# Layer 0's first shift and scale by TensorE in four column tiles instead of VectorE

## The chip, the cores and the metric

One core of a Trainium2 chip runs the whole program. The metric is the device time of one execution in microseconds (us); lower is better. Engines are called as the profile calls them: PE (TensorE) with its weight loads PEld, DVE (VectorE), ACT (ScalarE), POOL (GpSimd) and SP (SyncE, which here only issues transfers). Each engine runs its own instructions in its own order and waits on semaphores for the others. Transfers are issued by SP, ACT and POOL; each of the three has its own queue on the same 16 DMA engines (q1 for SP, q10 for ACT, q0 for POOL).

## What is computed

A two-layer encoder over 256 tokens of width 1024, conditioned on a vector `c`. Only the start matters here:

```python
mod = jnp.einsum('bd,lde->lbe', jax.nn.silu(c), w_ada) + b_ada[:, None, :]
for layer in range(DEPTH):
    shift1, scale1, gate1, shift2, scale2, gate2 = jnp.split(mod[layer][:, None, :], 6, axis=-1)
    h = x * (1.0 + scale1) + shift1
    y = hybrid_mixer(h, positions, w_in[layer], w_out[layer], ...)
    x = layer_norm(DEEPNORM_ALPHA * x + (1.0 + gate1) * y, ln_w[layer, 0], ln_b[layer, 0])
    h = x * (1.0 + scale2) + shift2
    f = swiglu(...) if layer % 2 == 0 else moe_swiglu(...)
    x = layer_norm(DEEPNORM_ALPHA * x + (1.0 + gate2) * f, ln_w[layer, 1], ln_b[layer, 1])
```

For each layer six vectors of 1024 (shift, scale and gate, twice) are products of `silu(c)` with a 1024 x 6144 matrix. Layer 0 cannot begin its first projection before its first shift and scale (pieces 0 and 1) are there, and they take 8 MB of weights.

## The kernel before

**Tiles and names.** 128 partitions hold 128 tokens or 128 of the 1024 features. `x` holds both token blocks b = 0, 1. The features are taken in two halves q = 0, 1 of four blocks of 128 each. All large weights come through four buffers of 1 MB (`raw`, tag "raw", `RAW = 4`), in the order in which SP issues them; a load waits until the buffer's last reader is done.

**The vectors.** `ada_steps` makes shifts and scales on DVE. `sc` is `c` broadcast to all partitions and put through Silu by ACT. One step loads 1 MB of transposed weights (two blocks of 128 outputs) and DVE multiplies each block by `sc` and sums along the row: one 128x1024 instruction per block of 128 outputs (L324) and one small instruction that adds the bias (L325). `feed(n)` runs n steps. For layer 0 the main loop calls `feed(4)` ahead of each half q, which makes scale and shift of that half: four loads and eight of the long DVE instructions.

**The first half-projection.** For each q: `transposed` turns `x` into features by PE (eight transposes L300 per q), `affine` applies scale and shift from PSUM (DVE and ACT in turn, L293 and L291), and `split` makes a high and a low part of the result (ACT copies the high part, L254; DVE subtracts to get the low part, L255). The weights of the projection go through the same `split`. `channels(0)` then multiplies: per half q 48 products of 128x256 (L476 to L478), three for each of four feature blocks and four output blocks. The high part alone is enough for the first product; the low part is needed from the second on. The second half q = 1 accumulates onto the first.

**Next on the path.** While the products run, DVE makes two blocks of another vector, splits weights and prepares constants; ACT then runs a chain of small activations with table loads (constants, rotary tables, the gates from the first projection) and then casts the weights of the next projection (ORDER "05...": chunk 5 follows chunk 0).

**The order.** A scheduler places the instructions of each engine in a fixed order at build time; on the chip each engine keeps that order. Within an engine, what stands behind a waiting instruction waits too.

**The routing's constants.** `moe` copies eight columns of `small` to `of` (L952), about 600 us into the program; the scheduler had moved the copy to the front of DVE's order.

Of the kernel before, what the change touches and what calls it, by code (L numbers as in the profile page):

```python
# [8 lines left out]
F32 = mybir.dt.float32  # L9
# [4 lines left out]
AF = mybir.ActivationFunctionType  # L14
# [3 lines left out]
P = 128  # L18
S = 256
NB = S // P  # L20
# [37 lines left out]
PLACES = PACKED + 2 * P  # L58
SMALL = PLACES + 3 * NE
LEVELS = (1, 2, 4, 8, 16, 32)  # L60
# [11 lines left out]
def shape_constants():  # L72
# [24 lines left out]
    small[:, PLACES + NE:PLACES + 2 * NE] = [NE * S * 2] + [-e for e in range(1, NE)]  # L97
    small[:, PLACES + 2 * NE:] = ROWS
    return {
# [7 lines left out]
def lay_out(i):  # L107
# [4 lines left out]
    o["pos"] = n["positions"].reshape(NB, P).T  # L112
    o["w_ada"] = n["w_ada"].reshape(DEPTH, D, 6, KD, P).transpose(0, 2, 3, 4, 1).reshape(DEPTH, 6, KD // 2, 2, P, D).transpose(0, 1, 2, 4, 3, 5)
    o["b_ada_c"] = n["b_ada"].reshape(DEPTH, 6, KD, P).transpose(3, 0, 1, 2)
    cols = np.arange(3072)
# [37 lines left out]
def trunk(tc, a, dbg=None):  # L153
# [37 lines left out]
    sc = work.tile([P, D], F32, name="sc")  # L191
    nc.scalar.dma_start(sc, a["c"].to_broadcast([P, D]))
    small = const.tile([P, SMALL], F32, name="small")
# [7 lines left out]
    x = const.tile([P, NB, D], F32, name="x")  # L201
    nc.scalar.dma_start(x, a["x"].rearrange("(b p) d -> p b d", p=P))
    lnc = const.tile([P, DEPTH, 2, 2, KD], F32, name="lnc")
    lbr = work.tile([P, DEPTH, NH], F32, name="lbr")
# [103 lines left out]


    A.activation(sc, sc, AF.Silu)  # L310

    mods = {}

    def ada_steps(todo):

        for l, piece, k in todo:
# [5 lines left out]
            for i in range(2):  # L322
# [4 lines left out]

    ada = ada_steps([(0, p, k) for k in range(0, KD, 2) for p in (1, 0)]
                    + [(*lp, k) for lp in ((0, 2), (0, 4), (0, 3), (0, 5), (1, 1), (1, 0), (1, 2), (1, 4), (1, 3), (1, 5))
                       for k in range(0, KD, 2)])  # L330

    def feed(n):
        for _ in range(n):
            next(ada, None)
# [611 lines left out]
    def moe(xn, cw, cb, g2):  # L946
# [4 lines left out]
        ind, gate, rank = [of[:, NB * j:NB * j + NB] for j in range(3)]  # L951
        V.tensor_copy(of[:, 4 * NB - 1], slots[:, 0:NE])  # L952
        tops = []
# [410 lines left out]
    for l in range(DEPTH):  # L1364
        hT = halves_T(f"hT{l}")
        last = {}
        for q in range(2):
            if l == 0:
                feed(4)
                cw, cb = mods[0, 1], mods[0, 0]  # L1370
            for b in range(NB):
                last[q, b] = to_T(src[b], b, q, hT, cw, cb, act=l > 0)
            if l == q == 0:
                early = load_w(a["w_in"][0, 0, 0], "win")
# [61 lines left out]
```

## Time and profile before

| | us |
|---|---|
| three runs | 1504.81, 1507.10, 1508.26 (median 1507.1) |
| the profiled execution, its own time | 1508.05 |
| its span, first to last instruction | 1505.9 |
| PE, DVE, ACT, POOL busy | 1308.8, 931.9, 646.9, 50.6 |

The profiled execution is 0.95 us above the median of the three runs, and its own time is 2.15 us longer than its span. The profile gives for each engine when an instruction began and how long it ran, and for an idle time what released the engine. PEclk is the clock that was granted to PE as a share of full speed: 1.00 is the level of 2.4 GHz and 0.50 that of 1.2 GHz. The first such record in this trace is at 33.4 us; before it the level is read from the spacing of equal products.

### The profile page before, as it was taken

Reading aid. Unit: us, or ns where it says so; the run is one execution under the profiler, and the core shown is the slowest. Engines: PE = TensorE matmul, PEld = TensorE weight load, DVE = VectorE, ACT = ScalarE, POOL = GpSimd, SP = SyncE. Lnnn points to the kernel's source line nnn. Section 1 sums busy time; section 2 is a strip of 40 time slices with the busy share of each in tenths; the row PEclk is TensorE's granted clock in tenths of the full one; section 3 lists DMA queues with packets and bytes.
Section 4 is the critical chain, followed back from the end, with each engine's and each line's share of the span. In section 5 each row is a group of like instructions: output and inputs, shape, how many; then the busy total and the mean of one; then the engine's idle time right before and its main releaser. Section 6 shows DMA issues by size and latency. Waiting matters only on the chain. (4 is left out here: it accounts for less than half of the span.)

```text
span 1505.9 us, 26044 instructions
## 1 busy us (share of the span) xinstructions
PE 1308.8 (87%) x10378; PEld 976.1 (65%) x10378; DVE 931.9 (62%) x1756; ACT 646.9 (43%) x1144; POOL 50.6 (3%) x44
## 2 busy tenths in 40 slices
PE   3699879999979999899999899989888898888884
PEld 2688757877768887676566567656666565655551
DVE  6799888888887987774343555443443555343424
ACT  2647744444445684564333334442444244333310
POOL 0000021000050000200000000000000000000000
PEclk9799989999979999799999999989999999888886
DMA  9773247899935403689999999999899999999994
GB/s 353 285 278 113 96 157 264 322 343 351 339 113 180 155 29 105 266 292 356 417 419 420 418 418 390 418 418 378 352 418 417 419 396 418 418 420 418 418 419 170
DMA packets 68753, 481.05 MB, mean 319 GB/s; under 512 B 8720, under 2 KB 8848, under 8 KB 11152
## 3 DMA queue, kind: packets, MB, share of 16 engines
q1 hardware_dynamic: 66672, 473.61, 79.6%
q0 software_dynamic: 960, 3.15, 0.7%
q10 hardware_dynamic: 992, 2.56, 0.4%
q8 instruction: 83, 1.36, 0.4%
q14 instruction: 46, 0.38, 0.1%
HBM read 478.23 MB, written 1.05 MB: 318 GB/s over the span
## 5 line engine op out<-in xcount | busy, mean ns | idle before, releaser
L255 DVE TENSOR_TENSOR pair<-rawb,pair 128x1024 fp32r<-128x1024 f32 x150 | 177.1, 1221 | 94.3 <-ACT pair L254 93.3
L254 ACT CAST pair<-rawb 128x1024 fp32r<-128x1024 f32 x150 | 149.9, 1048 | 36.2 <-DMA rawb<-m_up 20.4
L250 PE MATMUL pa<-pair,xe 128*128 128x512 f32 x336 | 139.4, 415 | 11.2 <-DVE pair L255 11.2
L249 PE MATMUL pa<-pair,xe 128*128 128x512 f32 x336 | 140.2, 417 | 9.7 <-ACT pair L254 9.2
L255 DVE TENSOR_TENSOR pair<-ring,pair 128x1024 fp32r<-128x1024 f32 x102 | 120.2, 1225 | 34.4 <-ACT pair L254 33.7
L251 PE MATMUL pa<-pair,xe 128*128 128x512 f32 x336 | 136.9, 407 | 0.0
L324 DVE CUSTOM_DVE_ANT_0 wada<-wada,sc 128x1024 f32<-128x1024 f32 x96 | 114.9, 1218 | 2.3 <-DMA wada<-w_ada 2.3
L808 ACT ACTIVATE g_act<-pa 128x256 f32<-128x256 f32 x64 | 24.6, 385 | 201.2 <-PE pa L251 201.2
L1132 PE MATMUL pa<-rawb,xl 128*32 128x128 f32 (+1 forms) x2320 | 103.7, 306 | 8.0 <-DMA rawb<-m_up 8.0
L254 ACT CAST pair<-ring 128x1024 fp32r<-128x1024 f32 x102 | 100.8, 1046 | 17.6 <-DVE rs_y L270 11.8
L1132 PEld LDWEIGHTS pa<-rawb,xl 128*32 128x32 f32 (+1 forms) x2320 | 79.4, 121 | 26.6 <-DMA rawb<-m_up 10.4
L1137 ACT COPY pk<-pa 128x128 f32<-128x128 f32 (+1 forms) x84 | 23.8, 283 | 154.3 <-PE pa L1132 154.3
L249 PEld LDWEIGHTS pa<-pair,xe 128*128 128x128 f32 x336 | 67.7, 201 | 32.1 <-ACT pair L254 13.6
L250 PEld LDWEIGHTS pa<-pair,xe 128*128 128x128 f32 x336 | 67.9, 202 | 31.3 <-DVE pair L255 17.6
L809 DVE TENSOR_TENSOR g_act<-g_act,pa 128x256 f32<-128x256 f32 x64 | 26.7, 417 | 97.6 <-ACT g_act L808 97.4
L255 DVE TENSOR_TENSOR g_l<-pb,g_h 128x256 fp32r<-128x256 f32 x64 | 27.0, 422 | 96.3 <-ACT g_h L254 96.1
L1132 PE MATMUL pa<-ring,xl 128*32 128x128 f32 (+1 forms) x1712 | 74.2, 301 | 11.1 <-DMA ring<-m_up 11.1
L251 PEld LDWEIGHTS pa<-pair,xe 128*128 128x128 f32 x336 | 67.9, 202 | 13.7
L254 ACT CAST win<-win 128x1024 fp32r<-128x1024 f32 x48 | 49.9, 1055 | 56.9 <-PE acc L251 24.0
L250 PE MATMUL pa<-wup,hTf 128*128 128x512 f32 x176 | 70.1, 398 | 2.4 <-DVE wup L255 2.4
L1132 PEld LDWEIGHTS pa<-ring,xl 128*32 128x32 f32 (+1 forms) x1712 | 56.5, 119 | 23.5 <-DMA ring<-m_up 13.9
L249 PE MATMUL acc<-pair,g_h 128*128 128x512 f32 x168 | 71.1, 423 | 0.0
(325 smaller groups left out, 2777.1 us busy)
## 6 DMA issues: line engine op xcount, KB each, us to landing
rawb<-m_up SPq DMA_DIRECT2D x129, 1024.0 KB, 13.0
ring<-m_up SPq DMA_DIRECT2D x95, 1024.0 KB, 13.1
rawb<-m_dn SPq DMA_DIRECT2D x71, 1024.0 KB, 14.4
wada<-w_ada SPq DMA_DIRECT2D x48, 1024.0 KB, 6.7
ring<-m_dn SPq DMA_DIRECT2D x41, 1024.0 KB, 14.7
win<-w_in SPq DMA_DIRECT2D x24, 1024.0 KB, 5.5
wup<-f_up SPq DMA_DIRECT2D x22, 1024.0 KB, 5.6
fdn<-f_dn SPq DMA_DIRECT2D x11, 1024.0 KB, 6.6
```

The source lines that it names most:

```text
L249: T.matmul(ps, xh, wh, start=first, stop=False)
L250: T.matmul(ps, xh, wl, start=False, stop=False)
L251: T.matmul(ps, xl, wh, start=False, stop=last)
L254: A.copy(h, src)
L255: return V.tensor_sub(lo, src, h.bitcast(F32))
L324: V.tensor_tensor_reduce(wi, wi, sc, 1.0, 0.0, ALU.mult, ALU.add, c[:, i:i + 1])
L808: A.activation(g, p[:, 0:FB], AF.Silu)
L809: V.tensor_mul(g, g, p[:, FB:2 * FB])
L1132: T.matmul(ps[n * i:n * i + n, 0:w], xr[:, k], ws[k // 4][:, c:c + w], start=k == 0, stop=k == KD - 1)
L1137: A.copy(s, ps)
```

## The change

Pieces 0 and 1 of layer 0 are no longer made by `ada_steps`. A second copy of their weights lies untransposed in `w_ada0`: one tile of 128x2048 (1 MB) holds four blocks of 128 inputs by 512 outputs. `c` comes a second time as `cc`, one column per block of 128 inputs (128x8), goes through Silu, and is repeated 32 times per block into `ccs`. `first_mods(q)` makes for piece 1, then 0: two tiles, each with four f32 products that go to four column tiles of PE, 32 output partitions each (L332); ACT copies the 128x512 sum from PSUM to `mod_s` (L334); four products with `pick`, whose column is 1 in every 32nd partition, add the four column tiles and turn the row into columns (L337, here called picks); DVE adds the bias (L338). The load of `sc`, which later vectors still need, goes behind `x` in ACT's queue; `cc` takes its place at the head. `of`'s copy is kept in program order.

```diff
@@ trunk: loads
-    nc.scalar.dma_start(sc, a["c"].to_broadcast([P, D]))
+    cc = const.tile([P, KD], F32, name="cc")
+    nc.scalar.dma_start(cc, a["c_c"])
...
     nc.scalar.dma_start(x, a["x"].rearrange("(b p) d -> p b d", p=P))
+    nc.scalar.dma_start(sc, a["c"].to_broadcast([P, D]))
+    pick = small[:, PICK:PICK + NE]
@@ vectors
+    A.activation(cc, cc, AF.Silu)
+    ccs = s1("ccs").rearrange("p (k j) -> p k j", k=KD)
+    V.tensor_copy(ccs, cc[:, :, None].to_broadcast([P, KD, QD]))
     A.activation(sc, sc, AF.Silu)
 
-    mods = {}
+    mods = {(0, p): const.tile([P, KD], F32, name=f"mod0{p}") for p in range(2)}
+
+    def first_mods(q):
+
+        for piece in (1, 0):
+            ps = bank("pa")
+            for h in range(2):
+                w = raw("wada")
+                nc.sync.dma_start(w, a["w_ada0"][q, piece, h].rearrange("p k n -> p (k n)"))
+                for i in range(4):
+                    T.matmul(ps[QD * i:QD * i + QD], ccs[:, 4 * h + i], w[:, 512 * i:512 * i + 512], start=h == 0, stop=h == 1)
+            s = s2("mod_s", "aff")
+            A.copy(s, ps)
+            pm = bank("pc")[:, 0:4 * NE].rearrange("p (j e) -> p j e", e=NE)
+            for j in range(4):
+                T.matmul(pm[:, j], s[:, j * P:(j + 1) * P], pick, start=True, stop=True)
+            V.scalar_tensor_tensor(mods[0, piece][:, 4 * q:4 * q + 4], pm[:, :, 0], float(piece), bac[:, 0, piece, 4 * q:4 * q + 4],
+                                   op0=ALU.add, op1=ALU.add)
@@
-    ada = ada_steps([(0, p, k) for k in range(0, KD, 2) for p in (1, 0)]
-                    + [(*lp, k) for lp in ((0, 2), (0, 4), (0, 3), (0, 5), (1, 1), (1, 0), (1, 2), (1, 4), (1, 3), (1, 5))
+    ada = ada_steps([(*lp, k) for lp in ((0, 2), (0, 4), (0, 3), (0, 5), (1, 1), (1, 0), (1, 2), (1, 4), (1, 3), (1, 5))
                        for k in range(0, KD, 2)])
@@ moe
-        V.tensor_copy(of[:, 4 * NB - 1], slots[:, 0:NE])
+        tc.keep_in_program_order(V.tensor_copy(of[:, 4 * NB - 1], slots[:, 0:NE]))
@@ main loop
             if l == 0:
-                feed(4)
+                first_mods(q)
                 cw, cb = mods[0, 1], mods[0, 0]
```

The order of instructions changes on PE, DVE and ACT up to the end of the first projection; behind it the only difference is `of`'s copy. SP issues the same loads in the same sequence: four weight tiles for q = 0 (called w1 to w4 below), the first projection tile, four for q = 1 (w5 to w8), the second projection tile.

ACT's instructions from the first one, before (`small` is a tile of constants, `bac` the biases, `cup` a tile that gets zeros, `win` weights of the projection, `hTf` the output of `affine`):

```order
L192 DMA sc<-c 128x1024
L194 DMA small<-k_small 128x800
L200 DMA bac<-b_ada_c 128x96
L202 DMA x<-x 128x2x1024
L310 ACT_TABLE_LOAD
L310 ACTIVATE sc<-sc 128x1024
L445 ACTIVATE cup<-small 128x15 x4
L254 CAST win_213<-win 128x1024
L254 CAST win_216<-win 128x1024
L291 ACTIVATE hTf<-pa,mod_119,mod_113 128x128 x4
```

and with the change:

```order
L197 DMA cc<-c_c 128x8
L199 DMA small<-k_small 128x808
L205 DMA bac<-b_ada_c 128x96
L207 DMA x<-x 128x2x1024
L208 DMA sc<-c 128x1024
L317 ACT_TABLE_LOAD
L317 ACTIVATE cc<-cc 128x8
L471 ACTIVATE cup<-small 128x15 x3
L320 ACTIVATE sc<-sc 128x1024
L471 ACTIVATE cup<-small 128x15
L334 COPY mod_s<-pa 128x512 x2
L298 ACTIVATE hTf<-pa,mod_96,mod_97 128x128 x2
```

The load of `sc` has moved from the first to the fifth place, and its activation now stands ahead of the two copies of `mod_s`; the casts of `win` have moved behind them.

PE's instructions from the first one, with the change (before, this place holds the 16 transposes of `x` and then the products L476 to L478 without a break; those products are L502 to L504 now):

```order
L332 MATMUL pa<-wada,ccs 32x512 x9
L337 MATMUL pc<-small,mod_s 128x8 x4
L332 MATMUL pa<-wada,ccs 32x512 x3
L307 MATMUL pa<-small,x 128x128 x2
L332 MATMUL pa<-wada,ccs 32x512 x4
L307 MATMUL pa<-small,x 128x128 x2
L337 MATMUL pc<-small,mod_s 128x8 x4
L307 MATMUL pa<-small,x 128x128 x4
L502 MATMUL acc_258<-hT_116,win_262 128x256
L332 MATMUL pa<-wada,ccs 32x512 x4
L503 MATMUL acc_258<-hT_117,win_262 128x256
L504 MATMUL acc_258<-hT_116,win_262 128x256
```

The first picks stand ahead of three products of w3, of all of w4's and of the transposes, and the products of w5 already stand between the first and the second product of the projection.

PE at the end of the projection's first half, with the change (before, nothing but the products L476 to L478 stands here):

```order
L332 MATMUL pa<-wada,ccs 32x512 x4
L504 MATMUL acc_259<-hT_116,win_265 128x256
L502 MATMUL acc_260<-hT_116,win_265 128x256
L503 MATMUL acc_260<-hT_117,win_265 128x256
L504 MATMUL acc_260<-hT_116,win_265 128x256
L502 MATMUL acc_261<-hT_116,win_265 128x256
L503 MATMUL acc_261<-hT_117,win_265 128x256
L337 MATMUL pc<-small,mod_s 128x8 x4
L307 MATMUL pa<-small,x 128x128 x4
L504 MATMUL acc_261<-hT_116,win_265 128x256
L502 MATMUL acc_258<-hT_118,win_318 128x256
L502 MATMUL acc_259<-hT_118,win_318 128x256
```

The products of w8, the last weight tile, and the last four picks stand behind all but a handful of the 48 products of the first half.

## Rows read from the trace of the kernel before

**Rows 1.** Busy time by stretch: PE, PEld, DVE, ACT, POOL, PEclk, DMA share, GB/s.

```profile
15.00:20.00 5.00, 0.00 (x0) 0.00 (x0) 5.00 (x11) 0.00 (x0) 0.00 (x0) 1.00 1.01 418
...
640.00:900.00 260.00, 243.71 (x1749) 165.86 (x1748) 131.29 (x185) 109.30 (x176) 0.00 (x0) 1.00 0.97 391
```

**Rows 2.** Timeline of the start: start us, duration us, engine, line, [idle before, releaser].

```profile
0.73 0.41 ACTq L192 DMA_DIRECT2D sc<-c  x1
...
8.09 1.06 ACT L310 ACTIVATE sc<-sc 128x1024 f32<-128x1024 f32 x1 [3.82 <-DMA sc<-c]
13.09 0.53 ACT L445 ACTIVATE cup<-small 128x15 fp32r<-128x15 f32 x4 [3.94 <-DMA small<-k_small]
13.09 0.17 DVE L952 COPY of<-small 128x8 f32<-128x8 f32 x1 [11.95 <-DMA small<-k_small]
```

**Rows 3.** Timeline from the first half's vectors to its first product.

```profile
23.36 1.94 PE L300 MATMUL pa<-small,x 128*128 128x128 f32 x8 [23.36 <-DMA x<-x]
...
24.82 0.15 DVE L325 SCALAR_TENSOR_TENSOR mod<-mod,bac 128x2 f32<-128x2 f32 x1
...
28.59 1.29 DVE L255 TENSOR_TENSOR hT<-hTf,hT 128x512 fp32r<-128x512 f32 x2
...
29.38 0.78 PE L476 MATMUL acc<-hT,win 128*128 128x256 f32 x2
```

**Rows 4.** Timeline from the second half's last vector instruction to the next projection.

```profile
39.82 0.15 DVE L325 SCALAR_TENSOR_TENSOR mod<-mod,bac 128x2 f32<-128x2 f32 x1
...
42.63 1.29 DVE L255 TENSOR_TENSOR hT<-hTf,hT 128x512 fp32r<-128x512 f32 x2
...
43.17 1.01 PE L476 MATMUL acc<-hT,win 128*128 128x256 f32 x3 [5.97 <-ACT hT L254]
...
48.24 0.40 ACT L684 ACTIVATE dg<-small,conv_w 128x128 fp32r<-128x128 f32 x1 [2.93 <-DVE conv_w L255]
...
58.18 3.92 ACT L254 CAST win<-win 128x1024 fp32r<-128x1024 f32 x4
```

**Rows 5.** DMA of the first 24 us: total; SP's queue; issues (KB each, us to landing).

```profile
DMA packets 1745, 8.73 MB, mean 364 GB/s; under 512 B 320, under 2 KB 320, under 8 KB 1024
...
q1 hardware_dynamic: 801, 5.91, 62.7%
...
x<-x ACTq DMA_DIRECT2D x1, 1024.0 KB, 21.1
...
sc<-c ACTq DMA_DIRECT2D x1, 512.0 KB, 7.3
small<-k_small ACTq DMA_DIRECT2D x1, 400.0 KB, 11.9
bac<-b_ada_c ACTq DMA_DIRECT2D x1, 48.0 KB, 14.5
```

**Rows 6.** Busy time by stretch, columns as in rows 1.

```profile
40.20:47.00 6.80, 3.83 (x17) 3.74 (x18) 6.28 (x9) 5.07 (x11) 0.00 (x0) 0.50 0.68 223
...
598.00:610.00 12.00, 10.76 (x50) 9.78 (x50) 10.68 (x38) 5.66 (x11) 8.94 (x7) 0.58 0.98 410
```

**Rows 7.** Timeline of PE in the routing: products with eight columns, ten records.

```profile
600.84 2.30 PE L958 MATMUL pc<-rtr,hTr 128*128 128x8 f32 x10
```

**Rows 8.** One line of the code, ACT: duration ns least/median/most.

```profile
L346 ACT COPY gate<-pc x8: 565/585/592, 172.7 to 574.3; 128x512 f32<-128x512 f32 x8
```

**Rows 9.** Timeline of PE: four column tiles of 512 columns (eight records), and the next.

```profile
845.91 1.04 PE L1157 MATMUL acc<-rawb,pk_g 128*32 128x512 f32 x8
846.88 0.44 PE L815 MATMUL pb<-small,g_act 128*128 128x128 f32 x2
```

**Rows 10.** Timeline of PE: equal products before and after the first rise of the clock.

```profile
31.39 0.41 PE L478 MATMUL acc<-hT,win 128*128 128x256 f32 x1
31.60 0.41 PE L476 MATMUL acc<-hT,win 128*128 128x256 f32 x1
...
33.46 0.27 PE L476 MATMUL acc<-hT,win 128*128 128x256 f32 x1
33.57 0.28 PE L477 MATMUL acc<-hT,win 128*128 128x256 f32 x1
```

More of the change, by code (lines that the diff above doesn't have):

```diff
@@ L58 @@
 PLACES = PACKED + 2 * P
-SMALL = PLACES + 3 * NE
+PICK = PLACES + 3 * NE
+SMALL = PICK + NE
 LEVELS = (1, 2, 4, 8, 16, 32)
@@ L97, in shape_constants @@
     small[:, PLACES + NE:PLACES + 2 * NE] = [NE * S * 2] + [-e for e in range(1, NE)]
-    small[:, PLACES + 2 * NE:] = ROWS
+    small[:, PLACES + 2 * NE:PICK] = ROWS
+    small[:, PICK:] = (np.arange(P) % QD == 0)[:, None]
     return {
@@ L113, in lay_out @@
     o["w_ada"] = n["w_ada"].reshape(DEPTH, D, 6, KD, P).transpose(0, 2, 3, 4, 1).reshape(DEPTH, 6, KD // 2, 2, P, D).transpose(0, 1, 2, 4, 3, 5)
+    o["c_c"] = n["c"].reshape(KD, P).T
+    o["w_ada0"] = n["w_ada"][0, :, 0:2 * D].reshape(2, 4, P, 2, 2, 512).transpose(4, 3, 0, 2, 1, 5)
     o["b_ada_c"] = n["b_ada"].reshape(DEPTH, 6, KD, P).transpose(3, 0, 1, 2)
```

## The prediction

> **What bounds the kernel now.** I read the stretches first, to see where the change can act at all. From 640 us on the DMA engines are the limit (share 0.97, 391 GB/s) [rows 1]; those transfers start when the layers before are done, so time lost or won ahead of them is passed on whole. The instruction order differs only in the first 60 us, so I read the start there, instruction by instruction. `sc` has landed at 0.73 + 7.3 = 8.0 us; ACT then applies Silu (1.06 us); DVE first waits until 13.1 us for `small`, because `of`'s copy stands at its front [rows 2, 5], and then makes blocks of the vectors without a pause (busy 5.00 of 5.00 us while PE does nothing and the DMA engines move 418 GB/s) [rows 1]. `x` lands at 23.4 us, the first half's last vector instruction ends at 24.97 us and PE's first product starts at 29.38 us, 4.4 us later; the low part of the operand is done at 29.88 us, 4.9 us later [rows 3]. The second half's vectors end at 39.97 us, its low part at 43.92 us [rows 4]. Behind that DVE and ACT follow without slack: ACT waits for DVE's `conv_w` until 48.24 us and runs its chain to the casts at 58.18 us [rows 4], on which the next projection waits. So the path runs: transfers, DVE's vectors, `affine` and `split` of half 0, then DVE's vectors of half 1 beside PE's products, `affine` and `split` of half 1, ACT's chain. What the change is worth is how much earlier or later the low part of half 1 is done than 43.92 us.
>
> **Half 0: what ACT waits for.** The change takes sixteen long DVE instructions away and gives PE eight groups of four column-tile products, sixteen picks and four ACT copies. The step that decides is not among these: Silu of `sc` stands on ACT ahead of the copies of `mod_s`, and `sc` is now the last of ACT's loads. PE's first picks need the first copy, and behind these picks PE's order holds the rest of w3, `x`'s transposes and w4.
>
> When does `sc` land? Before, ACT's queue landed `sc`, `small`, `bac` and `x` at 8.0, 13.1, 16.2 and 23.2 us [rows 2, 5], so 5.0 us for `small`, 3.1 for `bac` with its 128 small pieces, 7.1 for `x`. `cc` also has 128 small pieces, so I charge it 3.1 us instead of the first 5.0 or so: `cc` lands at about 6, `small` at 11, `bac` at 14, `x` at 21, and `sc` 3.5 us (half of `x`'s 7.1) to 5.0 us later, 25 to 26 us. A second count agrees: until then SP's queue moves w1 to w4, the projection tile and w5 (6.3 MB), the other queues what they moved before (8.73 - 5.91 = 2.8 MB) [rows 5]; 9.1 MB at 418 GB/s are 22 us from a start near 2.9 us. I take 25.8 us. The Trainium skill, DMA: Bandwidth & Descriptors (Specifications), gives an HBM limit of about 358 GB/s for one core. This trace has 418 in the same stretch, so the measurement decides; by the page's figure `sc` would land, as an estimate, some 3.5 us later and the sum would rise by as much.
>
> From there, at durations of the rows: Silu 1.06 and a piece of `cup` to 27.0; copy 0.58 [rows 8] to 27.6. Four picks are eight records; ten such records took 2.30 us in a stretch granted 0.58 [rows 6, 7], so 0.21 each and 1.7 us for four at the low level (1.2 GHz), 0.85 at the high one: 29.3. A group of four column tiles takes 0.97 us at the high level until the next instruction starts [rows 9], 1.9 at the low one: w3's last three, 31.2. Two of eight transposes in 1.94 us [rows 3]: 31.7. The clock: products come 0.21 us apart until 33.4 us and 0.12 after [rows 10], a rise 4.0 us after PE started to work without a pause at 29.38; after 43.17 us it rose at 47.0 us [rows 4, 6], 3.8 us. PE starts at 27.7 here, so w4 falls around the rise: 1.0 to 1.9, to 32.8 or 33.6. Copy 0.6 to 0.7, picks 0.85 to 1.7, the bias 0.15 [rows 3] with waits: the first half's vectors are ready between 34.6 and 36.5 us, I take **35.2** against 24.97. The first product follows 4.4 us later, at **39.6**.
>
> The Trainium skill, TensorEngine Tiling (Array Packing) (Key Properties), says that a change of tiling mode drains TensorE, which speaks against mixing column tiles with full products as this change does. The trace bears it out in a small size: two passes of 0.45 us would be 0.90 against 0.97. By the passes alone the sum would be about 0.4 us lower.
>
> **Half 1.** Before w8's sum is ready PE now has 46 products (0.12 us each, 5.5), four groups (3.9), eight picks (1.7) and four transposes (0.5): 11.6 us at the high level. PE has then idled about 4 us; before, a pause that began at 37.2 us (5.97 us ahead of 43.17 [rows 4]) had brought the low level by 40.2 us [rows 6]. So I start it low, and a rise after 4.2 us costs 2.1 more. With 0.3 for waits on the copy and the bias: vectors at **53.6** us against 39.97. Low part 4.9 us later, 58.5 against 43.92. **Sum: +14.6 us.**
>
> **What lies beside it.** w6 can only be issued when w3's products are done at 31 us, which leaves the DMA engines idle from 26 us; w6 and w7 still land at about 36 and 38, before PE needs them at 41 and later. w8 now waits until DVE has split the projection tile (some 7 us behind the vectors, 42 us) and lands some 5 us later, 47 (2.5 us for 1 MB at 418 GB/s, and 2.3 us from issue to first bytes as for `sc`, 7.3 less 5.0); PE comes to it at 50. The second projection tile goes right behind it, lands by 50, is needed at 55. If such a cover goes, half 1 slips by what is missing. DVE's relief earns nothing, since DVE waits for PE. `of`'s copy no longer holds DVE back until 13.1 us, and costs 0.17 us [rows 2] in the routing, at most that. The products of half 1 and ACT's chain are the same as before and move with the low part.
>
> **Numbers.** The profiled execution had 1508.05 us; 1508.05 + 14.6 = 1522.65. It stood 0.95 above the median, so against the median of 1507.1 I say 1521.7.
>
> Bounds of this case: with `sc` at 24.0 us, the high level from 30 us on and kept through half 1, and 4.4 instead of 4.9 at the end, vectors are ready at 32.8, the first product at 37.1, half 1's vectors at 49.0, low part 53.4: +9.5, 1516.6. With `sc` at 27.5, the low level all through half 0 and 6 us into half 1: 38.0, 42.7 (the last transposes add 0.3), 57.6, 62.5: +18.6, 1525.7.
>
> **Rivals.** (a) *ACT is not held.* If `sc` is down by 22 us, ACT has copied before `x`'s transposes are done, and w4 and the picks set the first half: `x` at 21, transposes 0.5, w4 1.9, copy 0.7, picks 1.7, bias 0.25 make 26; first product 30.4, half 1's vectors 44.4, low part 49.3: +5.4, 1512.5. For it: ACT's queue has fewer bytes in front. Against: all five loads share one queue, in order, and `x` alone takes until 21. (b) *Not slower.* PE's groups run at the high level from the first, since it now works from 7 us on, and `sc` lands before `x`. It decides if both hold: `x` at 20, transposes 0.3, w4 0.97, copy 0.7, picks and bias 1.1 make 23; product 27.4, 11.9 more, low part 44.2: no change, 1507.4, or 1 us less if the end takes 3.95 us as it did before (39.97 to 43.92). Against: PE works in pieces of 2 us with pauses, and before such a start was at the low level. (c) *The slip is swallowed.* Waits for weight transfers of the feed-forward stage shrink when the start is late. Only transfers that run ahead on their own could do so; four buffers bind them to their readers. It gives 1507 to 1515. (d) *More.* Picks or tile groups wait for each other more than counted, or w8 comes late: over 1526.
>
> **How the numbers follow.** The forecast has 0.78, (a) 0.09, (b) 0.05, (c) 0.04, (d) 0.04. A measurement of this kernel tells about 0.2% (3 us) from no change. (a), (d) and half of (c) are slower too: 0.78 + 0.09 + 0.04 + 0.02 = 0.93. Of (b) 0.03 and of (c) 0.02 lie within 0.2%, 0.02 of (b) is faster. The range 1512.0 to 1527.0 takes in the forecast's bounds and most of (a).
>
> **What would show it.** Right: on ACT an idle time that ends with the landing of `sc` near 26 us, ahead of the first copy of `mod_s`; PE's first picks right behind it, the first product near 40 us at 0.21 us spacing, the second half's first product near 58 instead of 43.17, ACT's chain later by the same. Wrong: the copies of `mod_s` at 12 to 18 us, or a first product before 32 us; then (a) or (b) holds. If the second half's shift is there and the total is not, (c).

## The result, and the profile after

The changed kernel took 1520.33 us (median of five runs, 1519.24 to 1523.71) where the kernel before took 1506.12 us in the same comparison: a ratio of 1.0101, 95% interval 1.0079 to 1.0123, so it is slower, by 1%. (A ratio is estimated from all runs of both kernels, so it isn't exactly the quotient of the two medians.) Measured once more, with six runs, it took 1521.85 against 1506.04 us, ratio 1.0098 (1.0068 to 1.0128). The forecast was 1521.7 us, 14.6 us more than before; the two comparisons give 14.2 and 15.8 us more. The profiled execution of the changed kernel had 1520.07 us with a span of 1518.3.

ACT's timeline of the changed kernel (start us, duration us, engine, line, operation; in brackets the idle time before it and what ended it):

```profile
2.14 1.04 ACTq L207 DMA_DIRECT2D x<-x  x1
3.20 0.54 ACTq L208 DMA_DIRECT2D sc<-c  x1
...
26.38 1.06 ACT L320 ACTIVATE sc<-sc 128x1024 f32<-128x1024 f32 x1 [14.22 <-DMA sc<-c]
...
27.45 0.56 ACT L334 COPY mod_s<-pa 128x512 f32<-128x512 f32 x1
...
65.83 0.40 ACT L710 ACTIVATE dg<-small,conv_w 128x128 fp32r<-128x128 f32 x1 [3.04 <-DVE conv_w L262]
...
75.78 3.92 ACT L261 CAST win<-win 128x1024 fp32r<-128x1024 f32 x4
```

ACT stands idle for 14.22 us until `sc` has landed, with the first copy of `mod_s` behind that activation. The last `dg` and the casts of the next weights, which stood at 48.24 and 58.18 us [rows 4], are at 65.83 and 75.78: 17.6 us later, both of them.

PE's timeline of the same execution. L332 are the column-tile groups, L337 the picks, L502 to L504 the products; four column-tile products or four picks are eight records:

```profile
28.07 1.88 PE L337 MATMUL pc<-small,mod_s 128*128 128x8 f32 x8 [11.23 <-ACT mod_s L334]
29.87 1.93 PE L332 MATMUL pa<-wada,ccs 128*32 128x512 f32 x6
...
32.35 1.94 PE L332 MATMUL pa<-wada,ccs 128*32 128x512 f32 x8
...
34.99 1.88 PE L337 MATMUL pc<-small,mod_s 128*128 128x8 f32 x8
...
41.55 0.58 PE L502 MATMUL acc<-hT,win 128*128 128x256 f32 x1 [3.73 <-ACT hT L261]
42.06 1.94 PE L332 MATMUL pa<-wada,ccs 128*32 128x512 f32 x8
...
45.72 1.31 PE L332 MATMUL pa<-wada,ccs 128*32 128x512 f32 x8
...
53.43 0.28 PE L503 MATMUL acc<-hT,win 128*128 128x256 f32 x1
53.64 1.06 PE L332 MATMUL pa<-wada,ccs 128*32 128x512 f32 x8
54.64 0.38 PE L504 MATMUL acc<-hT,win 128*128 128x256 f32 x1
54.86 0.28 PE L502 MATMUL acc<-hT,win 128*128 128x256 f32 x1
...
55.45 1.02 PE L337 MATMUL pc<-small,mod_s 128*128 128x8 f32 x8
...
60.76 1.01 PE L502 MATMUL acc<-hT,win 128*128 128x256 f32 x3 [3.67 <-ACT hT L261]
...
66.64 0.34 PE L504 MATMUL acc<-hT,win 128*128 128x256 f32 x1
```

PE waits 11.23 us for ACT's copy, with the rest of w3 and w4 behind the picks that wait. The first product stands at 41.55 us instead of 29.38 [rows 3], the first one of half 1 at 60.76 instead of 43.17 [rows 4]. From the first picks on, half 0's groups and picks run at the low level: a group takes 1.93 us there and 1.06 at 53.64 us, the picks 1.88 and 1.02.

DVE's timeline: the biases that finish the vectors of each half, and the low parts:

```profile
36.91 0.16 DVE L338 SCALAR_TENSOR_TENSOR mod<-pc,bac 128x4 f32<-128x4 f32 x1 [6.76 <-PE pc L337]
...
56.51 0.16 DVE L338 SCALAR_TENSOR_TENSOR mod<-pc,bac 128x4 f32<-128x4 f32 x1 [7.50 <-PE pc L337]
...
60.22 1.29 DVE L262 TENSOR_TENSOR hT<-hTf,hT 128x512 fp32r<-128x512 f32 x2
```

The vectors are ready at 37.07 and 56.67 us, half 1's low part at 61.51, where it was 43.92 [rows 4].

The loads of the first 24 us (KB each, us from issue to landing):

```profile
x<-x ACTq DMA_DIRECT2D x1, 1024.0 KB, 20.5
...
sc<-c ACTq DMA_DIRECT2D x1, 512.0 KB, 23.2
...
bac<-b_ada_c ACTq DMA_DIRECT2D x1, 48.0 KB, 13.5
cc<-c_c ACTq DMA_DIRECT2D x1, 4.0 KB, 5.3
```

`sc` was issued at 3.20 us and landed at 26.4; before, it came first and landed at 8.0 [rows 5].

Two lines of the program, as the view of one line gives them (duration ns least/median/most, first and last start). The copies of the gates, and the sums at the end of the expert stage, in the changed kernel:

```profile
L372 ACT COPY gate<-pc x8: 565/586/592, 189.9 to 590.4; 128x512 f32<-128x512 f32 x8
...
L1142 DVE TENSOR_TENSOR x<-x,pc x32: 679/686/690, 854.2 to 1486.0; 128x512 f32<-128x512 f32 x32
```

and the second one in the kernel before:

```profile
L1116 DVE TENSOR_TENSOR x<-x,pc x32: 680/687/690, 835.2 to 1472.9; 128x512 f32<-128x512 f32 x32
```

The gate copies were at 172.7 to 574.3 [rows 8]: the slip is 17.2 us at the first and 16.1 at the last. The sums slip by 19.0 us at their first and 13.1 at their last. So what is lost at the start is carried through both layers, in this profile with 4.5 us less at the end than at the start.

### The profile page after: what moved, and what is told of

It reads as the page before. It is cut to its first block, busy times and chain, and to the rows that moved or that the text cites. A ratio compares the mean times of both kernels' runs of the same rounds, so it can differ in the third digit from the quotient of the medians.

```text
span 1518.3 us, 26216 instructions
## 1 busy us (share of the span) xinstructions
PE 1324.3 (87%) x10474; PEld 980.7 (65%) x10474; DVE 913.2 (60%) x1721; ACT 648.8 (43%) x1149; POOL 51.7 (3%) x44
## 3 DMA queue, kind: packets, MB, share of 16 engines
q0 software_dynamic: 960, 3.15, 0.7%
## 5 line engine op out<-in xcount | busy, mean ns | idle before, releaser
L261 ACT CAST pair<-ring 128x1024 fp32r<-128x1024 f32 x102 | 100.8, 1047 | 16.0 <-DVE rs_y L277 11.9
L351 DVE CUSTOM_DVE_ANT_0 wada<-wada,sc 128x1024 f32<-128x1024 f32 x80 | 95.9, 1216 | 3.0 <-DMA wada<-w_ada 3.0
L256 PEld LDWEIGHTS pa<-pair,xe 128*128 128x128 f32 x336 | 67.8, 202 | 32.5 <-ACT pair L261 14.6
L257 PE MATMUL pa<-wup,hTf 128*128 128x512 f32 x176 | 70.2, 399 | 2.4 <-DVE wup L262 2.4
L256 PE MATMUL pa<-wup,hTf 128*128 128x512 f32 x176 | 70.2, 403 | 0.2 <-ACT hTf L298 0.2
## 6 DMA issues: line engine op xcount, KB each, us to landing
rawb<-m_up SPq DMA_DIRECT2D x129, 1024.0 KB, 13.1
```

The costliest lines, as they stand in the source:

```text
L256: T.matmul(ps, xh, wh, start=first, stop=False)
L257: T.matmul(ps, xh, wl, start=False, stop=False)
L261: A.copy(h, src)
L351: V.tensor_tensor_reduce(wi, wi, sc, 1.0, 0.0, ALU.mult, ALU.add, c[:, i:i + 1])
```

## The experiments

Experiments 1 to 4 take parts of the change apart, 5 and 6 mix both ways of making the vectors, 7 to 9 try to make the mixture pay, and 10 to 12 repeat earlier kernels for a question that had stayed open. "Slip" below is the start of the four casts of the next weights on ACT against 58.18 us [rows 4].

**1. ACT not held.** The activation of `sc` goes behind the first projection's load in the program and keeps that place; nothing else changes.

```diff
-    A.activation(sc, sc, AF.Silu)
@@ main loop, behind the load of the first projection tile
+                tc.keep_in_program_order(A.activation(sc, sc, AF.Silu))
```

> The changed kernel with one ACT instruction moved: Silu of sc stands behind the casts of the first half's operand instead of ahead of the copies of mod_s. Theory A (ACT's in-order wait for sc holds PE): the first copy runs at about 14 us, x (landing near 22.6 us as in the changed kernel) becomes the limit, the first half's vectors are ready at about 28 us instead of 37.1, all else follows: about 9 us less, 1511 to 1512. Theory B (the wait only covers PE's own slow work, eight groups and sixteen picks at the low clock level): within 2 us of the changed kernel, 1518 to 1522. Theory C (the wait is the whole loss): back to the kernel before, about 1506.

Measured: 1510.91 us against 1504.58, ratio 1.0048 (1.0028 to 1.0069). The 14.2 us that the change cost in its own comparison have become 6.3. ACT's timeline of this run:

```profile
13.40 0.58 ACT L333 COPY mod_s<-pa 128x512 f32<-128x512 f32 x1 [1.31 <-PE pa L331]
25.12 0.58 ACT L333 COPY mod_s<-pa 128x512 f32<-128x512 f32 x1 [11.13 <-PE pa L331]
...
66.98 3.92 ACT L261 CAST win<-win 128x1024 fp32r<-128x1024 f32 x4
```

and two lines of DVE's, the bias that finishes half 1's vectors and half 1's low part:

```profile
47.73 0.16 DVE L337 SCALAR_TENSOR_TENSOR mod<-pc,bac 128x4 f32<-128x4 f32 x1 [7.51 <-PE pc L336]
...
51.43 1.30 DVE L262 TENSOR_TENSOR hT<-hTf,hT 128x512 fp32r<-128x512 f32 x2
```

The first copy is at 13.40 us instead of 27.45, the slip is 8.8 us instead of 17.6. Half of the loss was ACT's order, with the same work on every engine and the same loads. Where the other 8.8 us arise, the same trace tells: half 0's vectors are ready at 27.83 us, 2.9 us later than before (24.97), half 1's at 47.89, 7.9 us later (39.97), and half 1's low part is done at 52.73, 8.8 us later (43.92 [rows 4]). So 2.9 us arise ahead of half 0's vectors, 5.0 between these and half 1's vectors, and 0.9 in half 1's `affine` and `split`.

**2. `sc` second in the queue.** ACT's order stays, the load moves up behind `cc`.

```diff
     nc.scalar.dma_start(cc, a["c_c"])
+    nc.scalar.dma_start(sc, a["c"].to_broadcast([P, D]))
...
     nc.scalar.dma_start(x, a["x"].rearrange("(b p) d -> p b d", p=P))
-    nc.scalar.dma_start(sc, a["c"].to_broadcast([P, D]))
```

> The changed kernel with the load of sc second in ACT's queue, right behind cc, and all instructions else in the same order. Theory A: sc lands near 11 us, ACT is free for the copies, but x lands 3.5 us later than in the changed kernel, near 26 us, and the first half's vectors are ready near 31.5 us: 5 to 6 us less than the changed kernel, 1514 to 1516, and 3 to 4 us more than with Silu moved. Theory B: 1518 to 1522.

Measured: 1515.61 us against 1504.58, ratio 1.0078 (1.0054 to 1.0102), slip 11.05 us (casts at 69.23). ACT is free early here too, but `x` is now behind 512 KB more and lands at 3.15 + 23.1 = 26.2 us, and `x`'s transposes stand ahead of w4's group on PE. So the place of `sc` in the queue has its own price at either end.

**3. `of`'s copy alone**, in the kernel before.

```diff
-        V.tensor_copy(of[:, 4 * NB - 1], slots[:, 0:NE])
+        tc.keep_in_program_order(V.tensor_copy(of[:, 4 * NB - 1], slots[:, 0:NE]))
```

> The kernel before with the second part of the change alone: the copy to of keeps its place in the routing. DVE can start its vector work at 9.2 us instead of 13.2. Theory A (x's landing at 23.4 us ends last in the first half, weight tiles land just in time): 0 to 1 us less, 1505 to 1506. Theory D (DVE's late start is on the path): up to 4 us less, 1502.

Measured: 1504.63 us against 1504.58, ratio 1.0000 (0.9982 to 1.0018). DVE's first long instruction, its first bias and its first part of `affine`, from this run's timeline:

```profile
9.25 1.23 DVE L324 CUSTOM_DVE_ANT_0 wada<-wada,sc 128x1024 f32<-128x1024 f32 x1 [8.11 <-ACT sc L310]
...
16.47 0.16 DVE L325 SCALAR_TENSOR_TENSOR mod<-mod,bac 128x2 f32<-128x2 f32 x1 [2.17 <-DMA bac<-b_ada_c]
...
24.98 0.41 DVE L293 TENSOR_SCALAR hTf<-pa,mod,mod 128x128 f32<-128x128 f32 x1 [2.48 <-PE pa L300]
```

DVE starts 4 us earlier than the 13.2 us of the kernel before, and then waits 1.43 us for the next weight tile, 2.17 us for `bac` and 2.48 us for `x`'s transposes; the casts are at 58.67 (slip 0.5). In the kernel before, `affine` had waited 1.80 us for the same transposes. So in both kernels half 0's `affine` began when `x` had landed and was transposed, and not when DVE was free. This part of the change is worth nothing that can be told.

**4. All eight vector tiles first**, on top of experiment 1: half 1's groups no longer stand among half 0's products, and the loads of w5 to w8 stand ahead of the first projection tile's.

```diff
-                first_mods(q)
+                if q == 0:
+                    first_mods(0)
+                    first_mods(1)
```

> As the run with Silu moved, and both halves' vectors are made ahead of the projection: the eight weight tiles are loaded first, the projection's first tile behind them, and no column tiles stand among the products. Theory A with its second step (half 1's vectors wait behind 46 products and their mixing): half 1's vectors ready near 35 us, the products then run without a pause from about 38 to 52 us, ACT's chain is limited by their end: 1502 to 1507, 5 to 9 us less than with Silu moved alone. Theory B2 (the place among the products costs nothing): the same as with Silu moved, 1511.

Measured: 1506.23 us against 1504.58, ratio 1.0022 (0.9999 to 1.0046), slip 4.9 us (casts at 63.08). Half 1's vectors are ready at 38.45 us, earlier than before (39.97), but both halves' `affine`, `split` and products then come in one piece behind them. So this version takes away 3.9 of the 8.8 us of slip left in experiment 1, and 4.9 stay; the 1.65 us between the two medians have an interval of -0.2 to 6.9 us. It changes PE's order in both halves: w4's group no longer stands behind `x`'s transposes (half 0's vectors are ready at 24.82 us instead of 27.83), and w5 to w8 no longer stand among the products. The order of the loads changes with it. That PE's order has a part in the loss is shown, the share of each of its places is not. PE's busy time in this run (columns as in rows 1) from 18.4 us to 37.4 us, and one group and one set of picks inside that stretch:

```profile
18.40:37.40 19.00, 16.78 (x72) 6.81 (x72) 0.90 (x4) 2.12 (x4) 0.00 (x0) 1.00 1.01 418
```

```profile
33.68 1.94 PE L331 MATMUL pa<-wada,ccs 128*32 128x512 f32 x8
...
36.38 1.87 PE L336 MATMUL pc<-small,mod_s 128*128 128x8 f32 x8 [0.76 <-ACT mod_s L333]
...
47.07 0.30 PE L501 MATMUL acc<-hT,win 128*128 128x256 f32 x1
```

PE is busy 16.78 of 19.00 us and still at the low level at 36.38 us (no clock record of this trace lies there; the level is read from the durations). It rose at 47.07 us, 4.0 us after the products began at 43.06 and 5.0 us after the four transposes right ahead of them.

**5 and 6. Both ways mixed.** PE makes the shift, DVE the scale, in the first half alone (5) or in both (6). `x`'s transposes are kept behind the first half's groups and picks, `sc` is first in the queue again and `cc` second.

```diff
-        for piece in (1, 0):
+        for piece in (0,):
             ps = bank("pa")
             for h in range(2):
+                feed(1)
@@ 5
-    ada = ada_steps([(*lp, k) for lp in ((0, 2), (0, 4), (0, 3), (0, 5), (1, 1), (1, 0), (1, 2), (1, 4), (1, 3), (1, 5))
+    ada = ada_steps([(0, 1, 0), (0, 1, 2), (0, 1, 4), (0, 0, 4), (0, 1, 6), (0, 0, 6)] + [(*lp, k) for lp in ((0, 2), (0, 4), (0, 3), (0, 5), (1, 1), (1, 0), (1, 2), (1, 4), (1, 3), (1, 5))
@@ 6, the same list
+    ada = ada_steps([(0, 1, 0), (0, 1, 2), (0, 1, 4), (0, 1, 6)] + [(*lp, k) for lp in ((0, 2), (0, 4), (0, 3), (0, 5), (1, 1), (1, 0), (1, 2), (1, 4), (1, 3), (1, 5))
```

> A mixed version: in the first half PE makes the shift (piece 0, two column-tile groups and four picks, with the transposes of x kept behind them), DVE makes the scale; the second half is made by DVE alone, as before; the load of sc is first in its queue again and cc second. PE's part lies in its idle time before x lands at about 23 us and DVE loses four of its long instructions there. Theory D (in the first half the loads set the time, and DVE's spare time there is not used, because its next instructions stand behind x): first half's vectors at 24 to 25.5 us, second half's low part at 43 to 45, time as before, 1503 to 1508. Theory P (PE's way is dear wherever it stands: copy, picks and bias follow each other at the low level): vectors of the first half 2 to 4 us later, time 1506 to 1510.

> As the mixed version, and PE makes the shift of the second half too (two groups and four picks among the products of the first half), DVE the scale. Theory D (the second half of the kernel before is bound by DVE's chain of eight long instructions between 27 and 40 us, and PE has room behind the first half's products, 5.97 us of idle time): four long instructions of 1.15 us fall away, PE's two groups and picks take about 6 us of which most lies in that room; second half's low part at 39 to 41.5 us instead of 43.9, time 1500 to 1503 where before gives 1504 to 1507. Theory P (the groups among the products push the products, and the picks stand behind them): low part at 43 to 47, time 1504 to 1509.

Measured: (5) 1506.85 us against 1504.83, ratio 1.0017 (0.9994 to 1.0040); (6) 1505.15, ratio 1.0007 (0.9985 to 1.0029). Neither can be told from the kernel before. In 5 the vectors are ready at 23.31 us, so PE's way wasn't late, against theory P; but `x` landed at 25.2 us instead of 23.2, half 1's low part came at 47.98, and the slip is 2.9 us. In 6 the low part came at 48.37 us, later even than the 43 to 47 of theory P, and the slip is 4.5 us (the profiled execution, at 1515.27 us, was the longest of its twelve). PE's timeline of run 6, SP's, and DVE's:

```profile
40.52 1.07 PE L337 MATMUL pa<-wada,ccs 128*32 128x512 f32 x8
...
42.29 1.06 PE L342 MATMUL pc<-small,mod_s 128*128 128x8 f32 x8
```

```profile
33.87 0.33 SPq L335 DMA_DIRECT2D wada<-w_ada  x1
```

```profile
32.62 1.22 DVE L356 CUSTOM_DVE_ANT_0 wada<-wada,sc 128x1024 f32<-128x1024 f32 x1
```

w8 could only be issued at 33.87 us, when DVE's second long instruction of w5 had ended (33.84) and w5 had left its buffer: SP waited 7.8 us for that instruction, which stands behind half 0's `affine` and parts of its `split` in DVE's order. The projection tile left its buffer later still, its last split ended at 34.98. (In the changed kernel w8 did wait for that tile, until 43.73 us.) The group of w8 stands among the products at 40.52 us and the picks at 42.29, while DVE had its scale ready at 37.5 us.

**7. The mixture with the vector tiles loaded ahead of the projection tile**, `cc` first and `sc` second in ACT's queue, half 0's `affine` behind w7.

```diff
@@ main loop
+                    first_mods(0)
+                    def between():
+                        for b in range(NB):
+                            last[0, b] = to_T(src[b], b, 0, hT, cw, cb)
+                    first_mods(1, between)
```

> The mixed version (PE makes the shift of both halves, DVE the scale) with all eight vector tiles loaded ahead of the first projection tile, so that the second half's last tile no longer waits for the buffer that the projection tile holds; cc is loaded first and sc second, and x's transposes and the first half's affine stand behind the second half's first groups. Theory D (in the kernel before, DVE's unbroken chain from 13.2 to 43.9 us sets the second half's low part; PE's idle time before the first product can take half of the long instructions off it): eight of sixteen long instructions fall away, 9.2 us; the last vector tile lands at 28 to 30 us, second half's vectors at 33 to 35, low part at 37 to 41, the first projection ends 3 to 6 us earlier than before; time 1499 to 1503 where before gives 1505. Theory W (the time behind the first projection is set by loads that start no earlier, so an earlier end there is swallowed): low part at 37 to 41, but time 1503 to 1507. Theory P (PE's path of group, copy, picks and bias is late again): low part at 43 or later, time 1505 to 1510.

Measured: 1504.39 us against 1502.71, ratio 1.0002 (0.9986 to 1.0018). Half 1's vectors are ready at 37.22 us, 2.8 us earlier than before, but its low part only at 46.94, where theory D had it at 37 to 41. Between the two DVE makes four splits of projection weights and one long instruction, at 1.22 us each, among half 1's `affine` and `split`. (The buffer that the expectation names was a misreading of run 6: w8 had waited there for w5.) ACT's timeline of this run:

```profile
48.98 0.40 ACT L719 ACTIVATE dg<-small,conv_w 128x128 fp32r<-128x128 f32 x1 [2.62 <-DVE conv_w L262]
...
58.92 3.92 ACT L261 CAST win<-win 128x1024 fp32r<-128x1024 f32 x4
```

Slip 0.7 us. PE's first product is at 39.53 us, so that the products of both halves, which before were parted by 5.97 us of idle time [rows 4], now follow each other and end no earlier.

**8 and 9. Loads reordered again (8), and the convolution's taps first (8 and 9).** In 8 the loads go w1 to w6, projection tile, w7, w8; 9 has the taps' part alone, in the kernel before.

```diff
-        for t, src in ((lnc, a["ln_c"]), (lbr, a["lb"]), (mraw, a["k_masks"]), (conv, a["conv"]), (pos, a["pos"]), (bias, a["k_bias"]),
+        for t, src in ((conv, a["conv"]), (lnc, a["ln_c"]), (lbr, a["lb"]), (mraw, a["k_masks"]), (pos, a["pos"]), (bias, a["k_bias"]),
-        V.tensor_copy(masks, mraw)
+        done = split(wp[:, 0], wp[:, 1], conv[:, 0, 1, 0:CONV])
+        with tc.issue_after(done.ins):
+            V.tensor_copy(masks, mraw)
```

> The mixed version with the loads in the order w1 to w6, projection tile, w7, w8 (no tile waits for a buffer that the projection tile holds), w6 and w7 made by PE, w5 and w8 by DVE; the load of the convolution's taps stands first among the later loads, their split is written ahead of the masks' copy and the masks' copy behind it. The trace of the version before this one showed why its earlier second half gave nothing: ACT's last dg waits for DVE's split of the taps, which stood behind two long instructions and the masks' copy, and ACT's chain of table loads and casts behind dg, on which PE waits 7.5 us, began at 48.98 us instead of 48.24. Theory G (ACT's chain from dg to the casts of the next projection's weights sets the path; it starts with the taps' split on DVE): second half's low part at 39 to 42 us, taps' split at 42 to 45, casts of the next weights at 53 to 56 instead of 58.18, time 1499.5 to 1503 where before gives 1504. Theory W (what comes later waits for loads or for the products anyway): casts at 53 to 56 but time as before, 1503 to 1506.

> The kernel before with the taps' part alone: their load first among the later loads, their split written ahead of the masks' copy, the masks' copy behind it. Both theories: DVE's two long instructions still stand ahead of the taps' split, so the last dg starts 0.5 to 0.8 us earlier (the masks' copy is 0.62 us) and the time falls by no more than 1 us: no difference that can be told.

Measured: (8) 1508.04 us against 1505.57, ratio 1.0021 (0.9999 to 1.0043); (9) 1502.96, ratio 0.9980 (0.9963 to 0.9998). Of 8 neither theory was tested, since the low part did not come early (47.97 us; slip 2.7). DVE's timeline shows why:

```profile
38.89 0.16 DVE L353 SCALAR_TENSOR_TENSOR mod<-pc,bac 128x4 f32<-128x4 f32 x1 [3.16 <-PE pc L352]
...
39.78 1.22 DVE L366 CUSTOM_DVE_ANT_0 wada<-wada,sc 128x1024 f32<-128x1024 f32 x1
```

DVE's part of w8 stands behind the bias that waits for PE's picks, so DVE idles 3.16 us and half 1's last vector comes at 42.35 us. The same pattern as ACT's in the changed kernel, one engine further. In 9 the interval ends just below 1. Its profile shows the split of the taps 0.7 us earlier behind half 1's low part than before, as expected, but the low part itself came 0.7 us later, and three `dg` (0.99 us in all) now stand where one stood ahead of ACT's chain; the casts are at 58.76 us (slip 0.6). Since the profile shows no gain at the place of the edit, I don't count the 2.6 us as its effect. No version here beat the kernel before by anything that its profile explains.

**10 to 12. Repeats**, for the level of PE's clock in the first half: the changed kernel twice, the version of experiment 2 once, unaltered.

> The changed kernel once more, unaltered. Its first profile had PE at the low level all through the first half (groups 1.93 us, picks 1.88 us from 28.07 to 36.9), where the prediction had counted a rise; the version with sc second had its second picks at 1.06 us. Theory K (the level in the first half belongs to the order of the work): again 1.88 and 1.93 there, first half's vectors near 37, second half's near 56.7. Theory X (it differs from execution to execution): the second picks at about 1.0 in one of the repeats, first half's vectors at 35 to 36. Time by either 1516 to 1522 where before gives 1504 to 1506.

> The changed kernel a third time, for its profile alone. Theory K: groups 1.93 us and picks 1.88 us through the first half, as in the first profile. Theory X: in this or the other repeat the second picks take about 1.0 us.

> The version with sc second once more, for its profile alone. Theory K: the second picks of the first half at about 1.06 us again, first half's vectors near 30.8. Theory X: they may take 1.88 us, first half's vectors then near 31.6.

The changed kernel was the same in both repeats: second picks 1.88 us, first half's vectors at 36.77 and 37.19 us, slips 17.3 and 17.5. (Times: 1521.85 us, median of six, and 1520.08 in one run; the version with `sc` second 1515.73 in one run.) The version with `sc` second was not. Its second picks of the first half in the first profile:

```profile
29.59 1.06 PE L337 MATMUL pc<-small,mod_s 128*128 128x8 f32 x8
```

and in the second profile:

```profile
29.46 1.87 PE L337 MATMUL pc<-small,mod_s 128*128 128x8 f32 x8
```

with vectors at 30.84 and 31.53 us and slips of 11.05 and 12.5. So which level half 0 gets can differ between two executions of one kernel (theory X); in three of three profiles the changed kernel got the low one.

## Why the prediction was right, and where it was off

**`sc` and ACT: right, the landing in part by luck.** The prediction had `sc` land at 25.8 us, it landed at 26.4; it had the picks at 27.6, they came at 28.07. `cc` landed at 6.0, `small` at 11.7, `bac` at 15.2, `x` at 22.6, against 6, 11, 14 and 21. So `x` was 1.6 us late, and `sc` followed it in 3.8 us instead of the 4.8 that 25.8 stands for: two errors that nearly cancel. That ACT's order costs half of the slip is shown by experiment 1: the same loads and the same work, 8.8 us of slip less. The Trainium skill, DMA: Bandwidth & Descriptors (Specifications), states an HBM limit of about 358 GB/s for one core, by which the estimate for `sc` would have been 3.5 us later, 29.3. The run's 26.4 us speak for the trace's 418 GB/s, with one core running.

**Half 0: the cause right, one term too small.** From the first picks (28.07) to the ready vectors (37.07) it took 9.0 us; the prediction had 7.6 (27.6 to 35.2). The step that was off is "so w4 falls around the rise: 1.0 to 1.9" and the picks "0.85 to 1.7" behind it: no rise came. w4 took 1.94 us, the picks 1.88, the values that the ranges give for the low level. The prediction took a rise 4.0 us after 29.38 us from PE's products before [rows 10] and applied it to groups and picks. The 4.0 us were themselves misread, for PE had worked without a pause since the eight transposes ahead of these products, 5.6 us before the rise:

```profile
27.75 1.97 PE L300 MATMUL pa<-small,x 128*128 128x128 f32 x8 [2.45 <-ACT hTf L291]
```

That half 1 of the same trace gave 3.8 us was chance: counted from the first product, the runs of this case have from 1.2 to 6.0 us (last section).

The 9.0 us are 1.4 more than forecast; with 0.5 us from the later start that makes 1.9 us, 37.07 instead of 35.2. From there to the first product 4.48 us passed, 4.4 forecast.

**Half 1: right but for 1.1 us.** From the first product (41.55) to the vectors (56.67) 15.1 us, forecast 14.0. It did start low (the group at 42.06 us took 1.94), and the rise lies inside the group at 45.72 us (1.31 us), so 4.2 to 5.5 us after 41.55 where 4.2 were assumed. At the two spacings of the products in it the rise lies, as an estimate, near 46.3 us, some 4.7 us after 41.55, which costs about 0.25 us. The larger part lies in the groups. The product ahead of the group at 53.64 us takes 0.21 us until the next start and the one behind it 0.22, where products follow each other in 0.12, and the group itself takes 1.00 (53.64 to 54.64): 1.43 us for the three instead of 0.97 + 2 x 0.12 = 1.21. That is some 0.2 us per group above the prediction's price, 0.9 for four (an estimate from this one group). The two together account for the 1.1 us. Low part 4.84 us behind the vectors, forecast 4.9. Sum at the low part: +17.6 us instead of +14.6.

**The total.** The casts on ACT slip by the same 17.6 us as the low part, and so did the first gate copy by 17.2: the path was the one named. Rival (c), a slip swallowed in the feed-forward stage, did not come: 16.1 us are left at 574 us [rows 8]. The comparisons of medians give 14.2 and 15.8 us, 3.4 and 1.8 us less than the slip at the start; their intervals, 11.9 to 18.5 and 10.2 to 19.3 us, both take in 17.6. Single executions wander in the expert stage. Experiment 3 has the kernel before but for one copy, and its sums there read

```profile
L1116 DVE TENSOR_TENSOR x<-x,pc x32: 679/689/690, 839.2 to 1471.1; 128x512 f32<-128x512 f32 x32
```

which is 4.0 us later than the kernel before at the first and 1.8 earlier at the last, though its only change in the order is a copy of 0.17 us. In the first repeat of the changed kernel they read

```profile
L1142 DVE TENSOR_TENSOR x<-x,pc x32: 679/687/690, 853.9 to 1490.1; 128x512 f32<-128x512 f32 x32
```

with 18.7 us of slip at the first and 17.2 at the last, where the first profile had 19.0 and 13.1. Over three profiles of either kernel (before and experiments 3 and 9, whose casts stand within 0.6 us of it; the changed kernel and its two repeats) the mean slip is 17.1 us at the casts, 15.0 at the last gate copy, 17.0 at the first sums, 15.2 at the last and 14.5 in the span, while single profiles lie up to 4.5 us apart. So the forecast of 1521.7 was as close as it is partly by luck: 3.0 us were missing at the start, and about as much was given back later. Whether the program gives it back or chance does is open.

**What lies beside it: right.** DVE lost sixteen of its long instructions. The page's group of them in the changed kernel (count, busy us, mean ns, idle time before):

```profile
L351 DVE CUSTOM_DVE_ANT_0 wada<-wada,sc 128x1024 f32<-128x1024 f32 x80 | 95.9, 1216 | 3.0 <-DMA wada<-w_ada 3.0
```

The sixteen that went would be 19.5 us at this mean, and nothing came of it, since DVE waits for PE instead (6.76 and 7.50 us ahead of the last biases). `of`'s copy was worth nothing that can be told (experiment 3). The transfers stop for want of a buffer, as forecast from 26 us on; the stretch from 28 to 32 us (columns as in rows 1):

```profile
28.00:32.00 4.00, 3.94 (x15) 2.25 (x16) 0.16 (x1) 0.01 (x1) 0.00 (x0) 1.00 0.00 0
```

Nothing moved there (the column for the clock says nothing here, its first record in this trace is at 46.3 us), and PE still did not wait for w6 to w8 later. One thing here was too small: the price of mixing column tiles with full products was put at 0.4 us in all. With two passes of 0.45 and two products of 0.12 the group at 53.64 us and the product on each side of it would take 1.14 us; they took 1.43, so some 0.3 us per group at the high level, 1.2 for four groups. The Trainium skill, TensorEngine Tiling (Array Packing) (Key Properties), says that a change of tiling mode drains TensorE. Those 0.3 us agree with a drain at such a change, though the trace does not show it as one.

**The rivals.** Rival (a), ACT not held, was not what happened, but experiment 1 made it happen: its first picks at 16.72 us, its vectors at 27.83 us (forecast of the rival 26) and 6.3 us more than before (forecast 5.4). The nearness of these two totals is in part luck, since the rival had the low part at 49.3 us and it was done at 52.73. Rival (b), not slower, had rested on groups at the high level from the first; they were low in the first half of every version with PE's groups, but for the last picks in one profile. The loss that remains in experiment 1 lies in both halves, 2.9 us ahead of half 0's vectors and 5.9 behind them; experiment 4 takes 3.9 us of it away with another order on PE and of the loads, and what holds the other 4.9 is not taken apart further.

## What to carry to other kernels

When a load is moved back in its queue, follow it to the in-order engine that reads it, and then to whatever stands behind that reader: here one activation of 1.06 us, whose result DVE first read at 52.64 us in experiment 1, held the copies of `mod_s`, and through them PE, and half of the loss went away by writing that activation further down. Moving work from a busy engine to an idle one pays only if the busy one's chain was what the next stage waited for; here half 0's `affine` waited for `x` and not for DVE, in the kernel before already (1.80 us, and 2.48 in experiment 3). Experiments 6 to 8 took eight of the sixteen long instructions off DVE, and each time another in-order wait (PE's picks among the products, DVE's block behind PE's bias, ACT's `dg` behind DVE's taps) stood at the same place.

## What the runs showed that I had not expected

PE's level in a stretch of column-tile groups and picks could not be told from how busy it was. In experiment 4 it was busy 16.78 of 19.00 us and stayed at 1.2 GHz, in the changed kernel from 28.07 us on as well, three times of three; in experiment 2 it had risen by 29.59 us in one execution and not in the other. Under products of 128x256 the rise came anywhere from 1.2 us after the first of them (experiment 3, half 0) over 2.9 (experiment 1, half 1) and 4.0 (experiment 4, and half 0 of the kernel before) to 6.0 us (half 1 of the changed kernel, from 60.76 us to the line at 66.64 above; 5.9 in its first repeat). PE's timeline of experiment 3:

```profile
29.86 0.78 PE L476 MATMUL acc<-hT,win 128*128 128x256 f32 x2
...
31.02 0.35 PE L477 MATMUL acc<-hT,win 128*128 128x256 f32 x1
```

Behind the line at 31.02 the products come 0.12 us apart. Its order on PE is that of the kernel before, where the same products rose 4.0 us after the first. What makes the difference is not settled by these runs.

A load of 4 KB at the head of a queue is not small: `cc`, 128 pieces, landed 5.3 us after its issue. With `cc` ahead and `sc` second (experiment 2) `x` landed at 26.2 us, with `sc` first and no `cc` (the kernel before) at 23.2, and in experiment 5, with `cc` behind `sc`, `x` landed at 25.2. In the changed kernel, where `cc`'s 4 KB stand ahead of `x` in place of `sc`'s 512 KB, `x` landed at 22.6, only 0.6 us earlier than before. These are whole kernels whose other loads differ too, so 2 to 3 us for `cc` is an estimate that no run isolates.
